# Feed-forward down product as a seven-product 2x2 block multiplication (Winograd's form of Strassen) in two passes

## The chip, the cores and the metric

The kernel runs on one core of a Trainium2 chip. The metric is the device time of one execution in microseconds (us). A core has a matrix engine (TensorE, PE), a vector engine (VectorE, DVE), a scalar engine (ScalarE, ACT), GpSimd (POOL) and SyncE (SP, which issues loads here); sixteen DMA engines move data between HBM and the core's SBUF, and matmuls write to eight PSUM banks. Each engine runs its own list of instructions in the order in which the compiler wrote them; semaphores tie the lists together.

## What is computed

A two-layer decoder trunk over 512 tokens of width 1024 in float32. Each layer has a token mixer (latent attention in layer 0, a gated linear recurrence in layer 1), and then

```python
x = layer_norm(ALPHA * x + mixer(x))
h = x @ w_in                                # 1024 -> 2 * 2816
x = layer_norm(ALPHA * x + (silu(g) * u) @ w_down)   # g, u: halves of h; 2816 -> 1024
x = x + sigmoid(x @ w_gate) * (p @ w_proj)
```

The change concerns the product with `w_down`: 512 tokens x 2816 features times 2816 x 1024, once in each layer.

## The kernel before

**Float32 by three products.** Every operand of a matmul is split into a rounded high part and a low part: `split` (line 178) has ACT copy the value into a float32r tile (`hi`, line 179) and DVE subtract it from the source (`lo`, line 180). `mm3` (line 197) then issues hi·hi, hi·lo and lo·hi (lines 200 to 202). `split_dma` (line 182) makes the low part without DVE: ACT writes the high part (line 184) and its negative (line 185), and a DMA that POOL issues adds the source from HBM to it (line 186), an accumulating DMA.

**Storage.** SBUF tiles come from pools with fixed numbers of buffers: `big`, 14 slots of 8 KB per partition (`slot`, line 167); `ma` and `mb`, five buffers each of 4 KB (`mid`, line 171; `MID_BUFS`, line 49); weights in `raw` (three buffers), `whi` and `wlo` (five each), used by `unit` (line 188). A new tile waits until the buffer that it takes over has had its last reader. PSUM has eight banks: `ps` 3, `sc` 2, `tp` 2, `wg` 1 (line 51). A planner at compile time sets each engine's order: among ready instructions the one that stands first in the program, as far as the buffers allow.

**Gate and up product, `gate_up` (line 380).** This stage stands ahead of the change and already is a Winograd product. Blocks j = 2 to 21 each prepare weights in `prep` (line 389: two loads, two accumulating DMAs, sums on DVE) and run seven products of 12 matmuls of 256 columns in `block` (line 435). It leaves h = silu(g)·u, transposed (features on the partitions), in `hT`: five `big` slots and one `mb` tile for the last two of the 22 feature groups. Beside it the class `Winograd` (line 100) holds the stage's input in eight `big` slots, and x takes two.

**Down product, `ffn` (line 478).** All eight PSUM banks hold the output: four token tiles of 128 (t) by two column halves of 512 (n). For each of the 22 feature groups k a weight tile of 128 x 1024 is loaded and split (`unit`), the 512 tokens of that group are split into an `ma` tile (`hsplit`, line 485), and `part` (line 490) adds 4 x 2 x 3 matmuls of 128x512. The last three groups go token tile by token tile, so that the LayerNorm (`ln_half`, `ln_finish`, lines 324 and 330) of one tile runs beside the matmuls of the next. `ln_finish` defers the transposes of its rows; `flush` (line 310) issues them.

**What follows, `ple` (line 511).** It loads and splits p, runs p·w_proj (48 matmuls), then flushes and runs the gate product in token order through `rows` (line 351).

Of the kernel before, what the change touches and what calls it, by code (L numbers as in the profile page):

```python
# [20 lines left out]
F32 = mybir.dt.float32  # L21
F32R = mybir.dt.float32r
# [18 lines left out]
NF = DFF // P  # L41
# [6 lines left out]
T2 = 4  # L48
# [97 lines left out]
class Builder:  # L146
# [24 lines left out]
    def mid(self, shape, dt=F32, tag="ma"):  # L171
        return self.t4.tile(shape, dt, tag=tag, bufs=MID_BUFS[tag], name=self.nm(tag))
# [175 lines left out]
        return self.small([P, 4], tag="lnst", bufs=6)  # L348


    def rows(self, lhs, units, consume, cut=()):

        for t in range(NT):
# [122 lines left out]
        return hT  # L476

    def ffn(self, l, x, xT, ln):
        hT = self.gate_up(l, xT)
        gb = self.ln_params(ln, True)  # L480
        yT = Pair(self)
        acc = [(self.bank(f), self.bank(g)) for f, g in (("tp", "tp"), ("sc", "sc"), ("ps", "ps"), ("ps", "wg"))]
        NL = 3

        def hsplit(k):
            h = self.mid([P, 2, S], F32R)
            self.split(h[:, 0], h[:, 1], hT[k // 4][:, k % 4, :])
            return h[:, 0], h[:, 1]

        def part(k, t, h, w):  # L490
            for n in range(2):
                self.mm3(acc[t][n], [z[:, t * P:(t + 1) * P] for z in h],
                         [z[:, n * 512:(n + 1) * 512] for z in w], k == 0, k == NF - 1)

        for k in range(NF - NL):
            w, h = self.unit(self.i["ffn_w_down"][l, k]), hsplit(k)
            for t in range(NT):
                part(k, t, h, w)
        last = [(k, self.unit(self.i["ffn_w_down"][l, k]), hsplit(k)) for k in range(NF - NL, NF)]
        for t in range(NT):  # L500
            for k, w, h in last:
                part(k, t, h, w)
            self.flush()
            st = self.new_stats()
            for n in range(2):
                self.ln_half(x, t, n, acc[t][n], st)
            self.ln_finish(x, t, st, gb, yT.sink)
        return yT


    def ple(self, l, x, xT, last):
        nc = self.nc
        praw = self.mid([P, 2, S])
        nc.sync.dma_start(praw, self.i["p"][l])
        pT = (self.mid([P, 2, S], F32R), self.mid([P, 2, S], F32R))
        self.split(pT[0], pT[1], praw)
        pp = Rows(self)
        yT = None if last else Pair(self)
        for n in range(2):
            w = self.unit(self.i["ple_w_proj"][l, n])  # L520
            for t in range(NT):
                ps = self.bank()
                for k in range(2):
                    self.mm3(ps, [z[:, k, t * P:(t + 1) * P] for z in pT], [z[:, k * 512:(k + 1) * 512] for z in w], k == 0, k == 1)
                nc.scalar.activation(pp(t, slice(n * 512, (n + 1) * 512)), ps, AF.Copy)
        self.flush()
        for n in range(2):
            def fin(t, c, ps):
                sg = self.small([P, 512], tag="t2", bufs=T2)[:, c]
                c = slice(n * 512 + c.start, n * 512 + c.stop)  # L530
                nc.scalar.activation(sg, ps, AF.Sigmoid)
# [7 lines left out]
            self.rows(xT, [self.unit(self.i["ple_w_gate"][l, n, u]) for u in range(4)], fin, (NT - 1,) if last and n else ())  # L539
        return yT  # L540


# [196 lines left out]
    def hgrn(self, xT):  # L739
# [9 lines left out]
        for n in range(2):  # L749
            def fin(t, c, ps):  # L750
                a_.activation(vv(t, slice(n * 512, (n + 1) * 512)), ps, AF.Copy)
            self.rows(xT, [self.unit(i["hgrn_w_v"][n, u]) for u in range(4)], fin)

        on = Rows(self)
        W2 = 4 * P
# [146 lines left out]
def layouts(x, p, positions, mla_w_dqkv, mla_q_norm, mla_kv_norm, mla_w_uq, mla_w_ukv, mla_w_o,  # L902
            hgrn_w_in, hgrn_lb_logits, hgrn_out_norm, hgrn_w_o, ffn_w_in, ffn_w_down,
            ln_mix_g, ln_mix_b, ln_ffn_g, ln_ffn_b, ple_w_proj, ple_w_gate):
    a = np.asarray
    c = np.ascontiguousarray
    order = token_order()
    x, p, positions = a(x)[0][order], a(p)[:, 0][:, order], a(positions)[0][order]
    o = {}
    o["x"] = c(x.reshape(NT, P, D).transpose(1, 0, 2))  # L910
    o["xT"] = c(x.T.reshape(KC, P, S).transpose(1, 0, 2))
    o["p"] = c(p.transpose(0, 2, 1).reshape(DEPTH, 2, P, S).transpose(0, 2, 1, 3))
    o["positions"] = c(positions.reshape(NT, P).T)
# [60 lines left out]
```

## Time and profile before

| | |
|---|---|
| median of 3 runs (lowest to highest) | 1300.67 us (1299.48 to 1301.2) |
| the profiled execution: its time, its span | 1299.13 us, 1297.0 us |
| granted TensorE clock | 0.999 |
| down product, layer 0: first matmul | 413.67 us after the span's start |
| down product, layer 0: window 413.67 to 534.00 us | 120.3 us, PE busy 120.3 us |

Times inside the trace count from the start of the span. "Busy" is the time in which an engine had an instruction running; a matmul's recorded length (0.39 us for 128x512) is longer than the distance from one to the next, since they are pipelined, so costs on PE are taken from distances. A wait's "releaser" is the event that ended it, inferred from semaphores.

### The profile page before, as it was taken

What the parts mean: (1) busy time and instruction counts of PE and PEld (TensorE: products, weight loads), DVE (VectorE), ACT (ScalarE), POOL (GpSimd) and SP (SyncE); (2) the same over time, 40 slices, a digit from 0 to 9 for tenths busy, and PEclk for the clock granted to TensorE, in tenths of its full rate; (3) what the DMA queues carried; (4) which work ended last, traced back from release to release, by engine and by line L of the source; (5) the groups of instructions that cost most, each with busy time, mean ns of one, the idle gap of its engine ahead of it and who ended that gap; (6) DMA issues with size and microseconds to landing.
All of it is one profiled execution on the core that took longest, in us unless ns stands there. A gap on an engine that the chain in (4) does not pass through costs nothing.

```text
span 1297.0 us, 20093 instructions
## 1 busy us (share of the span) xinstructions
PE 1272.0 (98%) x7900; PEld 1134.2 (87%) x7900; DVE 809.7 (62%) x1452; ACT 658.5 (51%) x1140; POOL 154.7 (12%) x167
## 2 busy tenths in 40 slices
PE   8999999999999999999999999999999999999998
PEld 8788889999999888888888887888999999888887
DVE  7998488677675332943377776449777676433463
ACT  6666357767764222533334344327767765422352
POOL 0200041111110000100002220023111111000000
PEclk9999999999999999999999999999999999999999
DMA  7213027877884323232412120323888786323231
GB/s 228 68 63 131 26 89 180 210 181 175 186 187 136 98 98 114 85 109 65 133 62 66 66 78 21 115 80 86 213 205 186 181 186 164 119 97 98 94 98 49
DMA packets 47614, 156.45 MB, mean 121 GB/s; under 512 B 5664, under 2 KB 5920, under 8 KB 47264
## 3 DMA queue, kind: packets, MB, share of 16 engines
q1 hardware_dynamic: 36000, 123.71, 29.7%
q0 software_dynamic: 11520, 31.46, 14.0%
q8 instruction: 62, 1.02, 0.3%
q14 instruction: 32, 0.26, 0.1%
HBM read 153.05 MB, written 2.10 MB: 120 GB/s over the span
## 4 chain that ended last, share of the span: by engine, by line
PE 83%; DVE 7%; DMA 4%; ACT 3%; issue 2%; POOL 1%; SPq 0%; DVEq 0%; ACTq 0%; POOLq 0%
PE ps L200 18%; PE ps L201 18%; PE ps L202 18%; PE sc L200 3%; DMA raw<-ffn_w_in 3%; PE sc L201 3%; PE sc L202 3%; PE wg L201 2%; PE wg L200 2%; PE wg L202 2%; PE tp L304 2%; PE sc L812 2%; PE tp L201 2%; PE tp L202 2%; PE tp L200 2%
## 5 line engine op out<-in xcount | busy, mean ns | idle before, releaser
L180 DVE TENSOR_TENSOR wlo<-raw,whi 128x1024 fp32r<-128x1024 f32 (+1 forms) x123 | 148.4, 1209 | 206.2 <-ACT whi L179 204.5
L179 ACT ACTIVATE whi<-raw 128x1024 fp32r<-128x1024 f32 (+1 forms) x135 | 139.5, 1038 | 230.1 <-PE wg L202 125.7
L200 PE MATMUL ps<-big,whi 128*128 128x256 f32 (+1 forms) x768 | 236.9, 308 | 0.0
L202 PE MATMUL ps<-big,wlo 128*128 128x256 f32 (+1 forms) x768 | 236.7, 308 | 0.0
L201 PE MATMUL ps<-big,whi 128*128 128x256 f32 (+1 forms) x768 | 235.5, 307 | 0.0
L200 PE MATMUL ps<-whi,big 128*128 128x512 f32 (+2 forms) x440 | 170.6, 388 | 1.0 <-ACT big L179 1.0
L202 PE MATMUL ps<-whi,big 128*128 128x512 f32 (+2 forms) x440 | 168.2, 382 | 0.0
L201 PE MATMUL ps<-wlo,big 128*128 128x512 f32 (+2 forms) x440 | 168.0, 382 | 0.0
L201 PEld LDWEIGHTS ps<-big,whi 128*128 128x128 f32 x768 | 146.8, 191 | 5.4
L202 PEld LDWEIGHTS ps<-big,wlo 128*128 128x128 f32 x768 | 146.8, 191 | 5.2
L200 PEld LDWEIGHTS ps<-big,whi 128*128 128x128 f32 x768 | 146.9, 191 | 4.8
L200 PEld LDWEIGHTS ps<-whi,big 128*128 128x128 f32 x440 | 82.9, 188 | 15.4 <-ACT big L179 1.2
L202 PEld LDWEIGHTS ps<-whi,big 128*128 128x128 f32 x440 | 82.7, 188 | 15.6
L201 PEld LDWEIGHTS ps<-wlo,big 128*128 128x128 f32 x440 | 82.9, 188 | 14.4
L210 POOL TENSOR_TENSOR rr<-rv,mhalf 128x1 f32<-128x1 f32 (+2 forms) x28 | 26.6, 951 | 481.3 <-DVE rv L208 481.3
L180 DVE TENSOR_TENSOR wlo<-ma,whi 128x1024 fp32r<-128x1024 f32 x40 | 49.0, 1224 | 34.2 <-ACT whi L179 34.2
L202 PE MATMUL ps<-whi,ma 128*128 128x512 f32 x164 | 64.2, 392 | 0.0
L201 PE MATMUL ps<-wlo,ma 128*128 128x512 f32 x164 | 64.2, 392 | 0.0
L200 PE MATMUL ps<-whi,ma 128*128 128x512 f32 x164 | 64.0, 390 | 0.0
L186 POOL DMA_DIRECT2D ma<-ffn_w_in x40 | 34.8, 870 | 234.4 <-DVE big L460 150.8
L439 ACT ACTIVATE part<-ps 128x256 f32<-128x256 f32 x120 | 44.5, 374 | 25.3 <-PE ps L202 24.8
L180 DVE TENSOR_TENSOR mb<-ma,mb 128x1024 fp32r<-128x1024 f32 x40 | 48.9, 1222 | 6.3 <-ACT mb L179 3.4
(309 smaller groups left out, 3071.8 us busy)
## 6 DMA issues: line engine op xcount, KB each, us to landing
raw<-ffn_w_in SPq DMA_DIRECT2D x88, 512.0 KB, 4.6
raw<-ffn_w_down SPq DMA_DIRECT2D x44, 512.0 KB, 3.5
wlo<-ffn_w_in POOLq DMA_DIRECT2D x40, 512.0 KB, 7.3
ma<-ffn_w_in POOLq DMA_DIRECT2D x40, 256.0 KB, 7.0
raw<-ple_w_gate SPq DMA_DIRECT2D x16, 512.0 KB, 3.5
raw<-hgrn_w_fq SPq DMA_DIRECT2D x16, 512.0 KB, 3.5
raw<-mla_w_o SPq DMA_DIRECT2D x8, 512.0 KB, 3.6
raw<-hgrn_w_v SPq DMA_DIRECT2D x8, 512.0 KB, 4.4
```

Source lines behind the costliest of these rows:

```text
L179: self.nc.scalar.activation(hi, src, AF.Copy)
L180: (eng or self.nc.vector).tensor_tensor(out=lo, in0=src, in1=hi.bitcast(F32), op=ALU.subtract)
L186: self.nc.gpsimd.dma_start(lo, src, accum_op=ALU.add)
L200: mm(ps, a[0], b[0], start=start, stop=False, skip_group_check=more)
L201: mm(ps, a[0], b[1], start=False, stop=False, skip_group_check=more)
L202: mm(ps, a[1], b[0], start=False, stop=stop, skip_group_check=more)
L210: nc.gpsimd.tensor_tensor(out=r, in0=v, in1=self.mhalf[:, :n], op=ALU.pow)
L304: self.nc.tensor.transpose(out=ps[:, c * P:(c + 1) * P], in_=src[:, c * P:(c + 1) * P], identity=self.ident)
L439: copy = lambda dst, src: nc.scalar.activation(dst, src[:, :N], AF.Copy)
L812: nc.tensor.matmul(ps[:, c * P:(c + 1) * P], X[:, c * P:(c + 1) * P], pair_view(cs[0][:, :, 1, :], cs[1][:, :, 0, :]), start=True, stop=True)
```

## The change

The 512 x 2816 by 2816 x 1024 product is cut in 2 x 2 blocks: A by token halves (tiles 0, 1 and 2, 3) and feature halves (groups 0 to 9 and 20; 10 to 19 and 21), B by the same feature halves and by column halves. With

S1 = A21 + A22, S2 = S1 - A11, S3 = A11 - A21, S4 = A12 - S2, T1 = B12 - B11, T2 = B22 - T1, T3 = T2 - B11, T4 = T2 - B21

the seven products are P1 = A11·B11, P2 = A12·B21, P3 = S4·B22, P4 = A22·T4, P5 = S1·T1, P6 = S2·T2, P7 = S3·T3, each 256 x 1408 by 1408 x 512 in two PSUM banks.

Pass 1 runs P5, P1, P6, P7 over the features in six blocks b of two group pairs (the block b = 5 has one), in the order 0, 1, 5, 2, 3, 4; all eight banks are in use. T1 and T2 are made by ACT (a negated copy) and an accumulating DMA from HBM (`minus`), the low part of B11 as well (`given`); T3 on DVE. T2 is kept for pass 2: the first in an `ma` tile, the others two by two in a `big` slot (`room`). Then P5 and P1 are copied out by ACT, and DVE forms q = P6 + P1 and c = P7 + q, in four `ma` tiles. Pass 2 runs P4, P2, P3 in the order 5, 0, 1, 2, 3, 4, with T4 on DVE; behind its second block DVE adds what pass 1 gave into x (`early`, 12 instructions). The last two blocks are closed token tile by token tile, first tiles 2 and 3 (P4), then 0 and 1 (P2 and P3). `ple`'s gate product and the value product of layer 1 take the tiles in the order 2, 3, 0, 1, and the array `w_down` is laid out in column halves.

```diff
     def ffn(self, l, x, xT, ln):
+        nc, v = self.nc, self.nc.vector
         hT = self.gate_up(l, xT)
+        wd = self.i["ffn_w_down"][l]
+        NB = 6
+        size = lambda b: 2 if b < NB - 1 else 1
...
+        def minus(dst, z, add):
+
+            nc.scalar.activation(dst, z, AF.Copy, scale=-1.0)
+            nc.gpsimd.dma_start(dst, add, accum_op=ALU.add)
+
+        def made(z, b):
+            w = wt("whi", b), wt("wlo", b)
+            self.split(*w, z)
+            return w
+
+        def given(r, s, b):
+            w = mid(b, "mb", F32R), mid(b, "mb", F32R)
+            self.split_dma(*w, r, s)
+            return w
+
+        def part(ps, t, s, w, b, first, last):
+            for c in range(size(b)):
+                self.mm3(ps, [z[:, c, t * P:(t + 1) * P] for z in s], [z[:, c * 512:(c + 1) * 512] for z in w],
+                         first and c == 0, last and c == size(b) - 1)
+
+        two = lambda f, g: (self.bank(f), self.bank(g))
+        p1, p5, p6, p7 = two("tp", "tp"), two("sc", "sc"), two("ps", "ps"), two("ps", "wg")
+        T2_, room = {}, None
+        order = (0, 1, 5, 2, 3, 4)
+        for n, b in enumerate(order):
+            m = size(b)
+            first, last = n == 0, n == NB - 1
+            r11 = load(0, 0, b)
+            b11 = given(r11, src(0, 0, b), b)
+            hi, lo = (self.slot([P, 4, 2, 256], F32R)[:, :, :m] for _ in range(2))
+            a11, a21, a22 = act(0, 0, b), act(0, 1, b), act(1, 1, b)
+            self.split(hi[:, 0], lo[:, 0], a11)
+            t1 = mid(b, "ma")
+            minus(t1, r11, src(0, 1, b))
+            w1 = made(t1, b)
+            s1 = self.small([P, 2, 256], tag="t2", bufs=T2)[:, :m]
+            v.tensor_tensor(out=s1, in0=a21, in1=a22, op=ALU.add)
+            self.split(hi[:, 1], lo[:, 1], s1)
+            if n == 0:
+                t2 = mid(b, "ma")
+            else:
+                if n % 2:
+                    room = self.slot([P, 2, 1024])
+                t2 = room[:, (n + 1) % 2, :512 * m]
+            T2_[b] = t2
+            minus(t2, t1, src(1, 1, b))
+            w2 = made(t2, b)
+            v.tensor_tensor(out=a21, in0=a11, in1=a21, op=ALU.subtract)
+            v.tensor_tensor(out=a11, in0=s1, in1=a11, op=ALU.subtract)
+            self.split(hi[:, 2], lo[:, 2], a11)
+            t3 = mid(b, "ma")
+            v.tensor_tensor(out=t3, in0=t2, in1=r11, op=ALU.subtract)
+            w3 = made(t3, b)
+            self.split(hi[:, 3], lo[:, 3], a21)
+            for ps, k, w in ((p5, 1, w1), (p1, 0, b11), (p6, 2, w2), (p7, 3, w3)):
+                for t in range(2):
+                    part(ps[t], t, (hi[:, k], lo[:, k]), w, b, first, last)
+
+        keep = lambda: self.mid([P, 2, 512])
+        u, a, q, c = keep(), keep(), keep(), keep()
+        for z, ps in ((u, p5), (a, p1)):
+            for t in range(2):
+                nc.scalar.activation(z[:, t], ps[t], AF.Copy)
+        for z, y, ps in ((q, a, p6), (c, q, p7)):
+            for t in range(2):
+                v.tensor_tensor(out=z[:, t], in0=ps[t], in1=y[:, t], op=ALU.add)
+        p4, p2, p3 = two("sc", "sc"), two("ps", "ps"), two("ps", "wg")
...
+        def early():
+            for t in range(2):
+                add(2 + t, 0, c[:, t], scale=ALPHA)
+                add(2 + t, 1, c[:, t], scale=ALPHA)
+                add(2 + t, 1, u[:, t], stat=True)
+                add(t, 0, a[:, t], scale=ALPHA)
+                add(t, 1, q[:, t], scale=ALPHA)
+                add(t, 1, u[:, t])
+
+        work = []
+        gb = yT = None
+        for b in range(NB):
...
+            b = (5, 0, 1, 2, 3, 4)[b]
+            m = size(b)
+            r21 = load(1, 0, b)
+            t4 = T2_[b]
+            v.tensor_tensor(out=t4, in0=t4, in1=r21, op=ALU.subtract)
+            w4 = made(t4, b)
+            hi, lo = (self.slot([P, 4, 2, 256], F32R)[:, :, :m] for _ in range(2))
+            a12, a22, s2 = act(1, 0, b), act(1, 1, b), act(0, 0, b)
+            self.split(hi[:, 0], lo[:, 0], a22)
+            b21 = given(r21, src(1, 0, b), b)
+            self.split(hi[:, 1], lo[:, 1], a12)
+            b22 = made(load(1, 1, b), b)
+            v.tensor_tensor(out=s2, in0=a12, in1=s2, op=ALU.subtract)
+            self.split(hi[:, 2], lo[:, 2], s2)
+            prods = ((p4, 0, w4), (p2, 1, b21), (p3, 2, b22))
+            if len(work) < NB - 2:
+                for ps, k, w in prods:
+                    for t in range(2):
+                        part(ps[t], t, (hi[:, k], lo[:, k]), w, b, not work, False)
+            work.append((b, hi, lo, prods))
+            if len(work) == 2:
+                early()
         gb = self.ln_params(ln, True)
         yT = Pair(self)
...
+        for t in range(2):
+            close(t, 0)
+            add(2 + t, 0, p4[t], ALU.subtract, stat=True)
+            self.ln_finish(x, 2 + t, st[2 + t], gb, yT.sink)
+        for t in range(2):
+            close(t, 1, 2)
+            add(t, 0, p2[t], stat=True)
+            add(t, 1, p3[t], stat=True)
+            self.ln_finish(x, t, st[t], gb, yT.sink)
         return yT
...
-    o["ffn_w_down"] = c(a(ffn_w_down).reshape(DEPTH, NF, P, D))
+    o["ffn_w_down"] = c(np.stack([halves(a(ffn_w_down)[l]) for l in range(DEPTH)]))
```

`load` issues a plain load by SP into a `raw` tile; `src(i, j, b)` is block Bij's part in HBM, `act(i, half, b)` the part of `hT` with feature half i and token half `half`, and `close` runs the named products of the last two blocks for one token tile and then `flush`.

More of the change, by code (lines that the diff above doesn't have):

```diff
@@ L348, in new_stats, with rows @@
         return self.small([P, 4], tag="lnst", bufs=6)
-    def rows(self, lhs, units, consume, cut=()):
-        for t in range(NT):
+    def rows(self, lhs, units, consume, cut=(), order=range(NT)):
+        for t in order:
             n = 256 if t in cut else 512
@@ L478, in ffn, with src, act @@
     def ffn(self, l, x, xT, ln):
+        nc, v = self.nc, self.nc.vector
         hT = self.gate_up(l, xT)
+        wd = self.i["ffn_w_down"][l]
+        NB = 6
+        size = lambda b: 2 if b < NB - 1 else 1
+        def src(i, j, b):
+            return wd[j, 5 * i + b] if b < NB - 1 else wd[j, 10][:, i * 512:(i + 1) * 512]
+        def act(i, half, b):
+            k = 10 * i + 2 * b if b < NB - 1 else 20 + i
+            return hT[k // 4][:, k % 4:k % 4 + size(b), half * 256:(half + 1) * 256]
@@ new lines, in ffn, with load @@
+        raw = lambda b: self.wp.tile([P, 1024], F32, tag="raw", bufs=3, name=self.nm("raw"))[:, :512 * size(b)]
+        wt = lambda tag, b: self.wp.tile([P, 1024], F32R, tag=tag, bufs=5, name=self.nm(tag))[:, :512 * size(b)]
+        mid = lambda b, tag, dt=F32: self.mid([P, 1024], dt, tag)[:, :512 * size(b)]
+        def load(i, j, b):
+            r = raw(b)
+            nc.sync.dma_start(r, src(i, j, b))
+            return r
+        def minus(dst, z, add):
+            nc.scalar.activation(dst, z, AF.Copy, scale=-1.0)
+            nc.gpsimd.dma_start(dst, add, accum_op=ALU.add)
@@ new lines, in ffn @@
+        keep = lambda: self.mid([P, 2, 512])
[7 more added lines that the diff above has]
+        p4, p2, p3 = two("sc", "sc"), two("ps", "ps"), two("ps", "wg")
+        st = [self.new_stats() for _ in range(NT)]
@@ new lines, in ffn, with add @@
+        L, R = slice(0, 512), slice(512, 1024)
+        def add(t, n, z, op=ALU.add, scale=1.0, stat=False):
+            xs = x(t, (L, R)[n])
+            kw = {"accum_out": st[t][:, n:n + 1]} if stat else {}
+            v.scalar_tensor_tensor(out=xs, in0=xs, scalar=scale, in1=z, op0=ALU.mult, op1=op, **kw)
+        def early():
[6 more added lines that the diff above has]
+                add(t, 1, u[:, t])
@@ new lines, in ffn @@
+        work = []
[3 more added lines that the diff above has]
+            b = (5, 0, 1, 2, 3, 4)[b]
+            m = size(b)
+            r21 = load(1, 0, b)
[18 more added lines that the diff above has]
+                early()
@@ L480, in ffn @@
         gb = self.ln_params(ln, True)
         yT = Pair(self)
[L482 to L502, printed above, removed]
-            self.flush()
[L504 to L507, printed above, removed]
+        def close(t, *ks):
+            for k in ks:
+                for n in (NB - 2, NB - 1):
+                    b, hi, lo, prods = work[n]
+                    ps, _, w = prods[k]
+                    part(ps[t], t, (hi[:, k], lo[:, k]), w, b, False, n == NB - 1)
+            self.flush()
@@ L538, in fin @@
                     self.defer(xs, yT.sink, t, n)
-            self.rows(xT, [self.unit(self.i["ple_w_gate"][l, n, u]) for u in range(4)], fin, (NT - 1,) if last and n else ())
+            self.rows(xT, [self.unit(self.i["ple_w_gate"][l, n, u]) for u in range(4)], fin, (1,) if last and n else (), (2, 3, 0, 1))
         return yT
@@ L751, in fin @@
                 a_.activation(vv(t, slice(n * 512, (n + 1) * 512)), ps, AF.Copy)
-            self.rows(xT, [self.unit(i["hgrn_w_v"][n, u]) for u in range(4)], fin)
+            self.rows(xT, [self.unit(i["hgrn_w_v"][n, u]) for u in range(4)], fin, (), (2, 3, 0, 1))
         on = Rows(self)
```

## Prediction

> **What bounds the kernel now.** I read the page first: busy times, then the shares of the chain that ended last.
>
> ```profile
> span 1297.0 us, 20093 instructions
> ...
> PE 1272.0 (98%) x7900; PEld 1134.2 (87%) x7900; DVE 809.7 (62%) x1452; ACT 658.5 (51%) x1140; POOL 154.7 (12%) x167
> ...
> PE 83%; DVE 7%; DMA 4%; ACT 3%; issue 2%; POOL 1%; SPq 0%; DVEq 0%; ACTq 0%; POOLq 0%
> ```
>
> PE is busy 98% of the span and carries 83% of the chain. But those are means; the stage decides. The table by windows, cut for layer 0 into gate-up blocks, the two windows ahead of the down product, and the down product in halves:
>
> ```profile
> core 0: us, PE busy (x) PEld busy (x) DVE busy (x) ACT busy (x) POOL busy (x), PEclk, DMA share, GB/s
> 353.20:363.30 10.10, 10.10 (x87) 10.10 (x86) 7.24 (x14) 7.11 (x13) 1.75 (x2) 1.00 0.81 182
> ...
> 383.50:393.60 10.10, 10.10 (x86) 10.10 (x86) 5.01 (x11) 6.38 (x12) 1.74 (x2) 1.00 0.85 182
> 393.60:403.60 10.00, 10.00 (x86) 10.00 (x85) 5.25 (x10) 5.51 (x10) 0.00 (x0) 1.00 0.35 107
> 403.60:413.67 10.07, 10.07 (x86) 10.07 (x85) 6.78 (x12) 5.81 (x11) 0.00 (x0) 1.00 0.57 210
> 413.67:473.60 59.93, 59.93 (x267) 49.62 (x266) 20.80 (x25) 17.18 (x22) 0.00 (x0) 1.00 0.30 96
> 473.60:534.00 60.40, 60.40 (x273) 49.52 (x271) 26.33 (x44) 19.40 (x25) 1.98 (x2) 1.00 0.28 88
> ```
>
> In the down product PE never stops (59.93 of 59.93, 60.40 of 60.40), while DVE is busy 20.80 and 26.33 us, ACT 17.18 and 19.40, the DMA engines 0.30 and 0.28. So a matmul taken out here is worth its whole distance, until one of the other three is full. That distance comes from the timeline of PE: the same place of the loop (first matmul into an `sc` bank), one feature group apart.
>
> ```profile
> 415.06 0.39 PE L200 MATMUL sc<-whi,ma 128*128 128x512 f32 x1
> ...
> 420.50 0.39 PE L200 MATMUL sc<-whi,ma 128*128 128x512 f32 x1
> ```
>
> 24 matmuls in 5.44 us: 0.2267 us each. Waits on this side run the other way, ACT and SP waiting for room:
>
> ```profile
> ACT whi L179 <- PE wg L202: 125.7, 37, 4.2
> ...
> DVE ma L398 <- DMA raw<-ffn_w_in: 15.1, 10, 2.6
> ```
>
> ACT waited for PE to give buffers back (125.7 us). The second row matters below: in gate-up DVE came to a load too early 10 times, by up to 2.6 us.
>
> **The matmuls that go.** Before, 22 groups x 24 = 528 a layer. After, seven products x 11 group pairs x 2 token tiles x 3 = 462, of the same form (128x512 moving). 66 x 0.2267 = 14.96 us a layer, 29.9 us in both. This term is a count times a distance; it can only be given back through stalls.
>
> **What ACT and DVE get.** Prices from their timelines, where instructions stand back to back, so that distances count:
>
> ```profile
> 402.35 0.63 ACT L179 ACTIVATE ma<-big 128x512 fp32r<-128x512 f32 x1 [1.05 <-PE ps L202]
> 402.89 1.04 ACT L179 ACTIVATE mb<-ma 128x1024 fp32r<-128x1024 f32 x1
> 403.83 1.04 ACT L179 ACTIVATE whi<-raw 128x1024 fp32r<-128x1024 f32 x1
> ```
>
> ```profile
> 403.22 0.69 DVE L180 TENSOR_TENSOR ma<-big,ma 128x512 fp32r<-128x512 f32 x1
> 403.82 0.42 DVE L462 TENSOR_TENSOR part<-ps,part 128x256 f32<-128x256 f32 x1
> ...
> 404.49 1.22 DVE L180 TENSOR_TENSOR mb<-ma,mb 128x1024 fp32r<-128x1024 f32 x1
> 405.62 0.42 DVE L465 TENSOR_TENSOR mb<-part,part 128x256 f32<-128x256 f32 x1
> ```
>
> ACT: 0.54 us for 512 columns, 0.94 for 1024. DVE: 0.60 and 1.13. A full block of pass 1 costs ACT seven long instructions (B11 twice, T1 and T2 negated, three high parts) and four short ones: 7 x 0.94 + 4 x 0.54 = 8.7 us. DVE: three low parts and T3, four short low parts, S1 to S3: 4 x 1.13 + 7 x 0.60 = 8.7 us. PE: 48 x 0.2267 = 10.9 us. Both fit, at 80%. A full block of pass 2: ACT 4 x 0.94 + 3 x 0.54 = 5.4, DVE 3 x 1.13 + 4 x 0.60 = 5.8, PE 36 x 0.2267 = 8.2 us. So in steady state they cost nothing, being beside PE; without that cover pass 1 alone would put some 48 us a layer on the path.
>
> **The accumulating DMAs.** Three in a block of pass 1, one in pass 2. Rows from gate-up, which has the same kind (the instructions of line 186; the DMA queues between 353.2 and 393.6 us; the end of the last block's preparation):
>
> ```profile
> L186 POOL DMA_DIRECT2D wlo<-ffn_w_in x40: 857/870/1042, 194.5 to 1086.5; - x40
> ...
> DMA to landing us min/median/max: 5.5/7.2/9.3
> ```
>
> ```profile
> q0 software_dynamic: 1152, 3.15, 44.4%
> q1 hardware_dynamic: 1152, 4.19, 35.9%
> ```
>
> ```profile
> 384.78 1.04 ACT L185 ACTIVATE wlo<-whi 128x1024 fp32r<-128x1024 f32 x1
> ```
>
> ```profile
> 386.23 0.87 POOL L186 DMA_DIRECT2D wlo<-ffn_w_in  x1 [1.47 <-ACT part L439]
> ```
>
> From issue to landing 7.2 us, at most 9.3. On the engines, 0.444 x 40.4 us / 3.15 MB x 0.524 MB = 2.98 us for an accumulate of 512 KB, 0.359 x 40.4 / 4.19 x 0.524 = 1.81 us for a plain load. ACT's negation ended at 385.82, POOL issued at 386.23: a hand-over of 0.4 us. POOL issues 24 a layer x 0.87 = 21 us in a stage where it has nothing else until the LayerNorm rows; SP issues 18 loads instead of 22. Neither is on the path.
>
> The start is covered. The `w_down` loads began 39 us ahead of the stage:
>
> ```profile
> 374.52 24.63 SPq L191 DMA_DIRECT2D raw<-ffn_w_down  x5
> ```
>
> The last gate-up accumulate is issued at 386.23; from 393.6 on the DMA engines are at 0.35 and 0.57, DVE busy 12.0 and ACT 11.3 of 20.1 us (of which four units of the old down product fall away). The first block's chain, load, T1, T2, T3, is about 4 + 2 x (1 + 7.2) + 1.2 + 2.3 = 24 us long and can start at 375: in time for 413.67.
>
> Where it can break is buffers. **Place A**, pass 1: `big` has 14 slots, 2 hold x and 5 hold h, so 7 are free. The first three blocks take 2 each, `room` 1. The fourth block's T2 needs the second `room`; the first block's two slots go to the fourth block's own parts, so `room` waits until PE ends the second block, 2 x 10.9 = 21.8 us into the stage. PE wants that T2 after the half block (5.4) and P5 and P1 of the fourth (5.4), 10.9 us later. The chain is 1.04 negation + 0.4 + 7.2 landing + 1.06 high + 1.22 low = 10.9 us: no slack at the median, 2.1 short at 9.3, 5.1 short with another accumulate (2.98) in front. Bounds 0 and 5.1; I take 2.1, since this stage's DMA load is above the one that gave the median.
>
> The Trainium skill ("DMA: Bandwidth & Descriptors", section "Anatomy of one DMA — SWDGE (gpsimd) path") has a fit of 2.0 us plus bytes over 436 GB/s for a DMA on this path, 3.2 us for 512 KB; by it place A would have 4 us to spare and cost nothing, and the forecast would be 4 us lower. The trace, with 5.5 us as the least, speaks against using it for accumulates.
>
> **Place B**, pass 2. The additions of pass 1's results are on DVE:
>
> ```profile
> L327 DVE SCALAR_TENSOR_TENSOR big<-big,ps x22: 674/688/689, 142.7 to 1236.8; 128x512 f32<-128x512 f32 x22
> ```
>
> From the end of pass 1 DVE has c (2 x 0.60), the second block's slot-bound splits (4 x 0.60), `early` (12 x 0.69 = 8.3) and then the third block's low parts of T4 and A22 (1.7; 2.9 if T4 itself isn't made earlier): 13.6 to 14.8 us. PE comes to the third block after 18 + 36 matmuls, 12.2 us. It stalls 1.4 to 2.6 us; 4.9 if the second block's T4 and its low part (2.3) slip behind as well, 0 if `early` is put later. I take 2.0. Behind `early` in DVE's queue stand the low parts for the remaining blocks; DVE regains 8.2 - 5.8 = 2.4 us a block.
>
> At nothing: copying P5 and P1 out (four ACT copies) and q are covered by P6 and P7 of the last block (5.4 us); c (1.2) by P4 and P2 of the half block (2.7); uncovered they would be 1.2. The last tiles close 2.7, 2.7, 5.4 and 5.4 us apart instead of 4.1, with DVE's part a little smaller (6 additions for 8); the last LayerNorm is hidden as before by the 48 matmuls of `ple` (10.9 us), and the new token order has the early tiles first.
>
> Sum: 29.9 - 2 x (2.1 + 2.0) = 21.7 us off. The profiled execution took 1299.13 us, so 1277.4; it lies 1.5 us under the median of 1300.67, so about 1279 against the median. With both stalls at nothing 1270.8, with both at their upper bounds (10.0 a layer) 1290.8; its own range is 1272 to 1289.
>
> **Rivals.** *All hidden*: the planner fills every gap, 1270.8. For it: PE waited for no accumulate at all before. Against: slack of zero at place A.
>
> *The DMA engines become the bound*: a pass 1 block needs 3 x 2.98 + 1.81 = 10.75 us of them in PE's 10.9 us, a share of 0.99, where the rows show 0.81 and 0.85. If 0.85 is the most, the block takes 12.6 us, at 0.81 13.3. With the first block prepared ahead 4.5 blocks are exposed: 8 to 11 us a layer instead of A, so 1300.67 - 29.9 + 16 to 22 + 4 = 1291 to 1297, priced at 1294, up to 1302 if B adds to it. Against: pass 1's accumulates can run ahead into windows at 0.35 and 0.57, so that some 41 us of DMA work is left for 54 us.
>
> *ACT stands in line behind the accumulates* (slower). In gate-up only PE reads an accumulated tile; now ACT must split T1 and T2 right after landing, twice in every block, and what is behind in its list (negations, B11, the next block) waits too. ACT has 10.9 - 8.7 = 2.2 us of slack in a block and the gain is 14.96 / 5.5 = 2.7 us a block; beyond 4.9 us of waits in a block, 2.45 per accumulate, the change loses. At half of the median landing (3.6 us each) a block takes 8.7 + 7.2 = 15.9 us, 5.0 too long, 27.5 us a layer: 1300.67 - 29.9 + 55 = 1326. For it: the 10 waits of DVE on loads of up to 2.6 us show that the planned order can come to data too early. Against: the accumulate issued at 386.23 was for a block that PE began at 403.6, so preparation ran a block ahead; with weights two blocks deep, T1's landing lies before its split's buffer is free.
> The Trainium skill ("TensorE: Matmul & The Clock Gate", section "Architectural detail: the array is 16× 32×32, not 1× 128×128") says that ACT and DVE take their queues strictly first in, first out, which is the rule that speaks against this change; nothing in the trace contradicts it.
>
> That the change doesn't do what it says I leave at no chance: the matmuls are counted.
>
> **How the numbers follow.** Forecast 0.49; all hidden 0.12; DMA bound 0.17 (0.11 faster, 0.05 no change, 0.01 slower); ACT in line 0.22. About 0.2% (2.6 us) is what a measurement of this kernel can tell from no change. Faster by more: 0.49 + 0.12 + 0.11 = 0.72; within 0.05; slower 0.01 + 0.22 = 0.23. The range from 1270 to 1306 holds all but most of the last case.
>
> **What would show it.** Right: PE's matmul count down by 132; in pass 1 PE with one gap of about 2 us ahead of P6 of the fourth block, released by T2's low part, and one of about 2 us at the third block of pass 2, released by DVE; ACT and DVE busy near 80% in pass 1. All hidden: no gap. DMA bound: share above 0.9 throughout pass 1, landings well over 9 us, gaps of 2 us in every block. ACT in line: idle times of ACT ahead of the splits of T1 and T2 ended by a DMA, over 2.45 us each. I am wrong if PE loses over 10 us a layer, or if a gap shows at the start of the stage.

## The result, and the profile after

The changed kernel takes 1339.32 us (median of 4 runs, 1338.22 to 1340.34) against 1300.3 us for the kernel before on the same chip: a ratio of 1.03, 95% interval 1.0282 to 1.0318. The change costs 39 us where 22 us of gain were forecast. The rival on the slower side, "ACT stands in line behind the accumulates", had been priced at 1326 us.

The profiled execution took 1340.34 us. Its page, from the span, the busy times and the chain that ended last:

```profile
span 1338.5 us, 20202 instructions
...
PE 1267.8 (95%) x7768; PEld 1120.8 (84%) x7768; DVE 912.3 (68%) x1608; ACT 751.9 (56%) x1276; POOL 196.4 (15%) x215
...
PE 66%; DMA 10%; issue 9%; DVE 8%; ACT 5%; POOL 1%; SPq 0%; POOLq 0%; DVEq 0%; ACTq 0%
```

The matmuls fell by 132, as counted. But PE's share of the chain fell from 83% to 66%, DMA's rose from 4% to 10%, and "issue" (time in which an engine waited for nothing that the profile shows) from 2% to 9%: a tenth of the time is now landings that somebody waits for. The window of pass 1 of layer 0 (264 matmuls, into P5, P1, P6 and P7; the columns are those of the table by windows above):

```profile
418.39:502.12 83.73, 69.31 (x266) 52.77 (x265) 50.19 (x74) 48.19 (x69) 13.88 (x16) 0.92 0.63 126
```

264 matmuls at 0.2267 us would be 59.85 us; pass 1 takes 83.73. No engine is full: DVE is busy 50.19 us, ACT 48.19, the DMA engines 0.63. The waits of this window (engine, line, releaser: us in total, times, longest) say what PE is short of:

```profile
DVE ma L558 <- DMA big<-ffn_w_down: 22.7, 5, 7.1
...
ACT whi L179 <- DMA big<-ffn_w_down: 18.1, 5, 6.0
...
ACT whi L179 <- DMA ma<-ffn_w_down: 10.4, 3, 4.3
...
PE sc L200 <- ACT whi L179: 6.6, 3, 4.8
...
PE ps L200 <- ACT whi L179: 3.7, 2, 2.7
...
PE sc L201 <- DVE wlo L180: 2.1, 3, 0.8
ACT whi L179 <- PE wg L202: 2.0, 1, 2.0
PE ps L201 <- DVE wlo L180: 1.9, 3, 0.9
```

Read the first two rows of ACT first: ACT, ahead of the high part of T2 (`big`) and of T1 (`ma`), waited eight times for an accumulate, 28.5 us in all, 3.6 us each. PE waited for those same high parts (`sc` is P5, which takes T1; `ps` is P6, which takes T2). DVE, ahead of T3, waited for T2's landings as well (the row of line 558, 22.7 us). The row of `wg` is the other half of the picture: ACT waited for room only once. Before, waiting for room was its main wait; now it is hardly ever ahead. ACT's waits of this window have no row of line 509 at all: no negation waited for a raw load or for a buffer to put T1 or T2 in.

ACT's timeline shows the order that does it. `raw` to `ma` is T1's negation, `ma` to `big` T2's, and each `whi` is the high part of what has just landed:

```profile
459.28 1.04 ACT L509 ACTIVATE ma<-raw 128x1024 f32<-128x1024 f32 x1
...
466.39 1.06 ACT L179 ACTIVATE whi<-ma 128x1024 fp32r<-128x1024 f32 x1 [2.11 <-DMA ma<-ffn_w_down]
467.36 1.04 ACT L509 ACTIVATE big<-ma 128x1024 f32<-128x1024 f32 x1
...
474.18 1.06 ACT L179 ACTIVATE whi<-big 128x1024 fp32r<-128x1024 f32 x1 [3.74 <-DMA big<-ffn_w_down]
475.14 1.04 ACT L509 ACTIVATE ma<-raw 128x1024 f32<-128x1024 f32 x1
```

T1's negation of the next block stands in ACT's list behind T2's high part of this one, so the next accumulate can't be issued before this one has landed and been split. From negation to negation is 475.14 - 459.28 = 15.86 us, where PE needs 10.9. This chain closes on ACT alone: twice a negation with its hand-over to POOL (1.45 and 1.44 us; POOL issued at 460.73 and 468.80), a landing (5.66 and 5.38) and a high part (0.97 and 0.96). DVE's wait for the same landing of T2 hangs beside it. The landings themselves were better than forecast; for the 24 accumulates of line 510, four of them of half the size:

```profile
DMA to landing us min/median/max: 4.0/5.6/7.2
```

On PE's side, the end of the half block's P7 (`wg`) and P5 of the fourth block (`sc`):

```profile
446.36 0.39 PE L202 MATMUL wg<-whi,big 128*128 128x512 f32 x1
451.59 0.65 PE L200 MATMUL sc<-whi,big 128*128 128x512 f32 x1 [4.84 <-ACT whi L179]
452.85 0.79 PE L201 MATMUL sc<-wlo,big 128*128 128x512 f32 x1 [0.61 <-DVE wlo L180]
453.44 0.63 PE L202 MATMUL sc<-whi,big 128*128 128x512 f32 x1
453.87 0.63 PE L200 MATMUL sc<-whi,big 128*128 128x512 f32 x1
...
459.53 0.39 PE L200 MATMUL tp<-mb,big 128*128 128x512 f32 x1
459.75 0.39 PE L201 MATMUL tp<-mb,big 128*128 128x512 f32 x1
```

PE stood still for 5.23 us and then ran at half speed: 0.43 us from matmul to matmul at 453.44, 0.22 again at 459.53. The granted clock (the column behind POOL's) and the DMA share behind it agree:

```profile
446.60:452.00 5.40, 0.56 (x2) 0.19 (x1) 0.90 (x2) 1.52 (x2) 0.85 (x1) 0.98 0.97 181
452.00:456.00 4.00, 3.38 (x8) 2.48 (x8) 0.80 (x1) 3.97 (x6) 0.87 (x1) 0.50 0.39 58
```

So pass 1's excess of 23.9 us is made of PE's own waits for high and low parts (6.6 + 3.7 + 2.1 + 1.9 = 14.3 us), of 23 matmuls behind two of the gaps that stand 0.43 instead of 0.23 us apart (4.6 us), and of 5.0 us around the waits, where the distance from matmul to matmul is longer than the wait (5.23 us across one of 4.84). Gap and half speed at 446.36 together cost 7.4 us. The Trainium skill ("TensorE: Matmul & The Clock Gate", section "What's actually happening") says that the clock is halved after at least one idle window of about 3.4 us and is whole again after at least about as much sustained work. The trace agrees for the 5.23 us here, and the return took 5.1 us of work without a gap (453.44 to 458.56). The trace also has half speed without a gap of 3.4 us: distances of 3.07 and 1.65 us with one matmul between them (from 489.62 on) were followed by 11 slow matmuls. A single distance of 2.98 us (402.35 to 405.33, below) was followed by none.

Two smaller losses have the same root or lie beside it. At the end of gate-up, ACT takes up T2 of the first block, and behind it in its list stand copies of PSUM that PE needs. ACT's and PE's timelines:

```profile
396.86 1.06 ACT L509 ACTIVATE ma<-ma 128x1024 f32<-128x1024 f32 x1 [4.38 <-DMA ma<-ffn_w_down]
...
403.95 1.06 ACT L179 ACTIVATE whi<-ma 128x1024 fp32r<-128x1024 f32 x1 [2.71 <-DMA ma<-ffn_w_down]
404.92 0.64 ACT L439 ACTIVATE part<-ps 128x256 f32<-128x256 f32 x2
```

```profile
405.33 0.38 PE L200 MATMUL ps<-big,ma 128*128 128x256 f32 x1 [2.71 <-ACT part L439]
```

T2's negation reads T1, so it waited 4.38 us for T1's accumulate. T2's high part then waited 2.71 us for T2's, and PE 2.71 us for the copy right behind that. Pass 1 starts 418.39 us into the span, 4.7 later than before (413.67); 3.5 of them came here, and 1.3 us were there already at the same matmul 247 us into the span, ahead of gate-up, a place that varies from -1.2 to +2.1 us among the profiles of the runs below. And in pass 2, ACT's timeline again:

```profile
540.59 1.06 ACT L179 ACTIVATE whi<-raw 128x1024 fp32r<-128x1024 f32 x1 [5.16 <-DMA raw<-ple_w_proj]
541.56 1.13 ACT L335 ACTIVATE t<-big,lnst 128x1024 bf16<-128x1024 f32 x1
```

Here ACT waited for a load of the next stage's weights, while the square for the LayerNorm, which PE needs soon, stood behind it. The DMA engines were full at that point (e7 below moves the load that shares them):

```profile
530.00:540.00 10.00, 9.15 (x41) 7.27 (x40) 6.80 (x12) 2.45 (x3) 0.65 (x1) 1.00 1.03 331
```

The account of layer 0: 4.7 later at the start, 23.9 in pass 1, 7.8 in pass 2 (54.66 us against 46.9 for its 198 matmuls and the transposes of two token tiles), less 15.0 for the matmuls: 21.4 us; measured at the layer's end, 21.1. Layer 1: 6.7 + 24.1 + 4.9 - 15.0 = 20.7; measured 20.4. Together 41.5, the difference of the two spans (1338.5 - 1297.0).

### The profile page after: what moved, and what is told of

Same layout as the page of the kernel before. It is cut to its first block, busy times and chain, and to the rows that moved or that the text cites. A ratio compares the mean times of both kernels' runs of the same rounds, so it can differ in the third digit from the quotient of the medians.

```text
span 1338.5 us, 20202 instructions
## 1 busy us (share of the span) xinstructions
PE 1267.8 (95%) x7768; PEld 1120.8 (84%) x7768; DVE 912.3 (68%) x1608; ACT 751.9 (56%) x1276; POOL 196.4 (15%) x215
## 4 chain that ended last, share of the span: by engine, by line
PE 66%; DMA 10%; issue 9%; DVE 8%; ACT 5%; POOL 1%; SPq 0%; POOLq 0%; DVEq 0%; ACTq 0%
PE ps L200 16%; PE ps L201 16%; PE ps L202 16%; DMA big<-ffn_w_down 3%; DMA raw<-ffn_w_in 3%; PE sc L200 2%; PE sc L201 2%; PE wg L201 2%; PE sc L202 2%; PE wg L200 2%; PE wg L202 2%; DMA ma<-ffn_w_down 2%; DMA raw<-ple_w_proj 2%; PE tp L304 2%; PE sc L942 2%
## 5 line engine op out<-in xcount | busy, mean ns | idle before, releaser
L200 PE MATMUL ps<-whi,big 128*128 128x512 f32 (+2 forms) x528 | 208.6, 395 | 6.2 <-ACT whi L179 6.2
L201 PE MATMUL ps<-wlo,big 128*128 128x512 f32 (+2 forms) x528 | 205.8, 390 | 4.0 <-DVE wlo L180 3.9
L202 PE MATMUL ps<-whi,big 128*128 128x512 f32 (+2 forms) x528 | 205.1, 388 | 0.0
L179 ACT ACTIVATE whi<-raw 128x1024 fp32r<-128x1024 f32 (+1 forms) x103 | 104.7, 1022 | 102.3 <-PE ps L202 35.7
L180 DVE TENSOR_TENSOR wlo<-raw,whi 128x1024 fp32r<-128x1024 f32 (+1 forms) x91 | 108.3, 1192 | 73.5 <-ACT whi L179 71.9
L180 DVE TENSOR_TENSOR wlo<-ma,whi 128x1024 fp32r<-128x1024 f32 (+1 forms) x68 | 81.1, 1192 | 64.0 <-ACT whi L179 64.0
L200 PEld LDWEIGHTS ps<-whi,big 128*128 128x128 f32 x528 | 101.1, 192 | 26.2 <-ACT whi L179 8.3
L201 PEld LDWEIGHTS ps<-wlo,big 128*128 128x128 f32 x528 | 101.2, 192 | 25.4 <-DVE wlo L180 7.4
L202 PEld LDWEIGHTS ps<-whi,big 128*128 128x128 f32 x528 | 100.8, 191 | 19.1
L179 ACT ACTIVATE whi<-ma 128x1024 fp32r<-128x1024 f32 (+1 forms) x68 | 69.7, 1025 | 39.4 <-DMA ma<-ffn_w_down 28.7
L200 PE MATMUL sc<-whi,big 128*128 128x512 f32 (+1 forms) x104 | 42.1, 408 | 14.6 <-ACT whi L179 14.6
L180 POOL TENSOR_TENSOR wlo<-raw,whi 128x1024 fp32r<-128x1024 f32 x12 | 29.6, 2475 | 152.1 <-ACT whi L179 152.1
```

Source lines behind the costliest of these rows:

```text
L179: self.nc.scalar.activation(hi, src, AF.Copy)
L180: (eng or self.nc.vector).tensor_tensor(out=lo, in0=src, in1=hi.bitcast(F32), op=ALU.subtract)
L200: mm(ps, a[0], b[0], start=start, stop=False, skip_group_check=more)
L201: mm(ps, a[0], b[1], start=False, stop=False, skip_group_check=more)
L202: mm(ps, a[1], b[0], start=False, stop=stop, skip_group_check=more)
```

## The experiments

The theory: ACT's place in line. The landings of T1 and T2 lie in series on ACT, and a block takes ACT's own work plus two waits. The rivals: the DMA engines are full, and the loss would be there whoever waits; or the gaps come from buffers (place A); or ACT and DVE simply have too much work. The table holds all eight runs; "pass 1" is the distance from the first to the 265th matmul in layer 0 and layer 1.

| kernel | median us (runs) | ratio to before, interval | pass 1, us |
|---|---|---|---|
| changed | 1339.32 (4) | 1.03, 1.0282 to 1.0318 | 83.7, 84.0 |
| e1_cut | 1279.12 (2) | 0.9845, 0.9816 to 0.9873 | 59.9, 59.9 |
| e2_dve_sums | 1284.64 (2) | 0.9887, 0.9823 to 0.9952 | 59.9, 59.9 |
| e3_pool_sums | 1306.09 (4) | 1.0052, 1.0032 to 1.0072 | 68.0, 68.6 |
| e4_order | 1296.81 (8) | 0.9979, 0.9968 to 0.9991 | 67.2, 65.2 |
| e5_dve_ln | 1276.0 (4) | 0.9815, 0.9797 to 0.9832 | 59.9, 59.9 |
| e6_dve_ln_pool0 | 1275.91 (4) | 0.9815, 0.98 to 0.9831 | 59.9, 59.9 |
| e7_acc_ln | 1333.18 (2) | 1.0258, 1.0232 to 1.0283 | 83.6, 83.3 |
| e8_t1_dve | 1315.96 (2) | 1.0125, 1.0091 to 1.0159 | 69.3, 69.2 |

The kernel before, timed again beside e1 to e4, took 1299.44 us, beside e5 to e8 1300.04.

**e1_cut**: all instructions and DMAs stay, but nothing in pass 1 reads T1 or T2. (PE still reads B11's low part, which is accumulated too.)

```
-            w1 = made(t1, b)
+            w1 = made(r11, b)
...
-            minus(t2, t1, src(1, 1, b))
-            w2 = made(t2, b)
+            minus(t2, r11, src(1, 1, b))
+            w2 = made(r11, b)
...
-            v.tensor_tensor(out=t3, in0=t2, in1=r11, op=ALU.subtract)
+            v.tensor_tensor(out=t3, in0=r11, in1=r11, op=ALU.subtract)
```

> The same instructions and the same DMAs as the changed kernel, but in pass 1 no engine waits for a sum: the products P5 and P6 take B11's split in place of T1's and T2's, the negation for T2 reads B11 in place of T1, and T3 is B11 - B11 (so P5, P6 and P7 are not the reference's; T2 is still read in pass 2). Theory, ACT stands in line behind the accumulates: the 24 us that pass 1 loses in a layer and most of the 4.7 us ahead of it go, and the half clock behind the long gaps with them: 1339 - 2 x 28 = about 1283 us, pass 1 near its 60 us of matmuls. Rival 1, the DMA engines are full: their work is unchanged at 10.75 us in a block, so pass 1 stays at 75 us or more and the time at 1320 to 1339. Rival 2, buffers (room for T2, weights): they are unchanged too, so 1325 or more.

Measured 1279.12 us. Pass 1 of layer 0:

```profile
414.20:474.10 59.90, 59.90 (x267) 49.62 (x266) 51.31 (x76) 48.21 (x69) 13.91 (x16) 1.00 0.87 183
```

PE has no gap left, with the same work on ACT (48.21 us), DVE (51.31) and POOL, and with the same DMAs in less time: a share of 0.87. The buffers are as many, though T1's is free sooner, having no reader left. That buffers weren't it, ACT's waits above show (no row of line 509). So neither the DMA engines nor the amount of work made the loss; the reading of what was just accumulated did. Pass 1 starts at 414.2 instead of 418.39: the delay at gate-up's end goes with it. This is what the change would have brought if the landings of T1 and T2 had been hidden in pass 1. That it is the prediction's time as well is luck: its 8.3 us over the 1270.8 without stalls lie at neither place that the prediction priced, but late in pass 2 (51.2 and 51.0 us against 46.9), where PE itself waits 2.63 and 2.42 us for an accumulate (`mb`, B21's low part).

**e2_dve_sums**: T1 and T2 by a plain load and a subtraction on DVE.

```
         def minus(dst, z, add):
...
-            nc.scalar.activation(dst, z, AF.Copy, scale=-1.0)
-            nc.gpsimd.dma_start(dst, add, accum_op=ALU.add)
+            nc.sync.dma_start(dst, add)
+            v.tensor_tensor(out=dst, in0=dst, in1=z, op=ALU.subtract)
```

> T1 and T2 from plain loads (SP) and one subtraction on DVE each, in place of ACT's negated copy and the accumulating DMA. ACT loses 1.9 us in a block and waits for no accumulate, DVE gets 2.3 us more, 11.0 us in PE's 10.9; DMA work falls to 8.4 us. Theory (ACT in line): pass 1 near 62 to 66 us with DVE as its bound, 1290 to 1300 us in all. Rival 1 (DMA engines full) also expects a gain, of the share from 0.99 to 0.77: 1290 to 1310. Rival 2 (buffers): no gain, 1330 or more.

Measured 1284.64 us, two runs (1281.14 and 1288.15; the profile is of the second), less than any case expected. Pass 1 of layer 0:

```profile
413.54:473.41 59.87, 59.87 (x267) 49.56 (x265) 59.05 (x84) 40.42 (x60) 6.10 (x7) 1.00 0.64 180
```

DVE's 59.05 us fill the pass, and PE still has no gap: the plain load needs no predecessor, so it is issued as soon as its buffer is free, and the subtraction costs 1.2 us of an engine in place of a landing. What is left is at the ends. ACT's timeline in pass 2, and DVE's at the end of gate-up in layer 1:

```profile
511.79 1.06 ACT L179 ACTIVATE whi<-raw 128x1024 fp32r<-128x1024 f32 x1 [5.14 <-DMA raw<-ple_w_proj]
512.75 1.13 ACT L335 ACTIVATE t<-big,lnst 128x1024 bf16<-128x1024 f32 x1
```

```profile
1090.37 1.23 DVE L510 TENSOR_TENSOR ma<-ma,raw 128x1024 f32<-128x1024 f32 x1 [6.71 <-DMA ma<-ffn_w_down]
```

The first is the wait for `ple_w_proj` again. The second is the theory's own wait on another engine: in layer 1 DVE stood in line for 6.71 us ahead of the first block's T1, and gate-up's end came 1.9 us later by it.

**e3_pool_sums**: the same, with the subtractions on GpSimd.

```
+            nc.sync.dma_start(dst, add)
+            nc.gpsimd.tensor_tensor(out=dst, in0=dst, in1=z, op=ALU.subtract)
```

> As with the sums on DVE, but the two subtractions on GpSimd (2.5 us each by its low parts of 128x1024, 5 us of 10.9 in a block), which has nothing else in pass 1. ACT and DVE wait for GpSimd in place of a DMA: 2.5 us in place of 5.6. Theory: pass 1 near 61 to 64 us, 1282 to 1295 in all, below the version on DVE. Rival 2 (buffers): no gain. If DVE's instructions get longer beside GpSimd, both engines slow down and the time is 1300 or more.

Measured 1306.09 us, 0.5% slower than before. GpSimd's and DVE's timelines in pass 1:

```profile
440.36 5.38 POOL L510 TENSOR_TENSOR big<-big,ma 128x1024 f32<-128x1024 f32 x1
...
446.30 2.95 POOL L510 TENSOR_TENSOR ma<-ma,raw 128x1024 f32<-128x1024 f32 x1
449.33 2.71 POOL L510 TENSOR_TENSOR big<-big,ma 128x1024 f32<-128x1024 f32 x1
```

```profile
446.91 2.89 DVE L180 TENSOR_TENSOR big<-big,big 128x512 fp32r<-128x512 f32 x1
449.73 3.39 DVE L180 TENSOR_TENSOR wlo<-big,whi 128x1024 fp32r<-128x1024 f32 x1
453.04 1.21 DVE L180 TENSOR_TENSOR wlo<-ma,whi 128x1024 fp32r<-128x1024 f32 x1
454.17 0.68 DVE L180 TENSOR_TENSOR big<-t,big 128x512 fp32r<-128x512 f32 x1
```

The low part of 512 columns takes 2.89 us beside GpSimd and 0.68 alone, that of 1024 columns 3.39 and 1.21; GpSimd itself takes between 2.7 and 5.4 us in these rows for one shape. The two slow each other down, and the free engine wasn't free. The Trainium skill ("SBUF — State Buffer", section "SBUF: two separate sides") says that GpSimd and a VectorE instruction with two SBUF inputs take turns at a shared pair of ports, one waiting for the whole of the other's instruction; the rows agree, with 2.2 us of waiting in each.

**e4_order**: accumulates as in the change, but written down in another order: T1 of block n+2 and T2 of block n+1 are begun ahead of the splits of block n. To pay for the tiles kept longer, the half block's hi and lo share a slot.

```
+        one(0)
+        one(1)
+        other(0)
         for n, b in enumerate(order):
+            if n + 2 < NB:
+                one(n + 2)
+            if n + 1 < NB:
+                other(n + 1)
```

Here `one(n)` is the load of A11's block and T1's `minus`, `other(n)` the split of B11 and T2's `minus`.

> The sums stay accumulating DMAs, of the same number and size; only the order in the program changes: T1's negation and DMA stand two blocks ahead of the splits that need it, T2's and B11's one block ahead (the half block's parts share one slot, so that the buffers allow it). Theory (ACT in line): each landing of 5 to 7 us now lies behind a block of 10.9 us, so pass 1 falls to 62 to 68 us and the total to 1285 to 1305. Rival 1 (DMA engines full): the DMA work is the same 10.75 us a block, so pass 1 stays above 70 us and the total above 1320.

Measured 1296.81 us: faster than before by 0.2%, the interval just clear of none. Pass 1 of layer 0, and ACT's waits there:

```profile
413.08:480.29 67.21, 63.55 (x267) 51.40 (x265) 53.11 (x78) 46.69 (x69) 11.70 (x14) 0.95 0.76 160
```

```profile
ACT ma L509 <- DMA raw<-ffn_w_down: 6.6, 2, 4.4
ACT big L509 <- DMA ma<-ffn_w_down: 4.8, 3, 3.0
```

With the same accumulates, the same DMA work and the same operations, the order (with the slot that it needs) takes 42 of the 60 us that lie between the changed kernel and e1_cut. The slot alone wasn't run. The rest lies in both passes, 12.6 us over e1 in pass 1 and 8.5 in pass 2: in pass 1 ACT now stands in line elsewhere, ahead of the negations, for the raw load (6.6 us) and for T1 (4.8), and in pass 2 of layer 0 PE waits 5.3 us for the accumulate of B21's low part.

**e8_t1_dve**: T1 by a plain load and DVE, T2 by the accumulate: one landing a block instead of two.

```
-            minus(t1, r11, src(0, 1, b))
+            nc.sync.dma_start(t1, src(0, 1, b))
+            v.tensor_tensor(out=t1, in0=t1, in1=r11, op=ALU.subtract)
```

> The changed kernel with T1 alone from a plain load and a subtraction on DVE; T2 stays an accumulating DMA. ACT has one wait for an accumulate in a block in place of two in series. Theory (two landings in series on ACT set the 15.9 us of a block): a block takes 8 to 12 us of ACT's chain, pass 1 falls from 84 to 62 to 70 us, and the time to 1288 to 1310. Rival (the wait for T2 alone decides, since T3 on DVE hangs on it as well): pass 1 stays above 75 us, 1320 or more.

Measured 1315.96 us, more than the 1288 to 1310 expected, and pass 1 69.25 us, as expected. ACT's timeline, from high part of T2 to the next full block's, and its waits:

```profile
450.98 1.06 ACT L179 ACTIVATE whi<-big 128x1024 fp32r<-128x1024 f32 x1 [2.13 <-DMA big<-ffn_w_down]
...
464.24 1.06 ACT L179 ACTIVATE whi<-big 128x1024 fp32r<-128x1024 f32 x1 [3.43 <-DMA big<-ffn_w_down]
```

```profile
ACT whi L179 <- DMA big<-ffn_w_down: 18.0, 5, 5.9
```

The block takes 13.26 us with one landing in line, where 8 to 12 were expected, against 15.87 with two between the same instructions (458.31 to 474.18), and with none PE's 10.9 decide. T2's wait is as large as in the changed kernel (18.0 and 18.1 us). T1's landing (10.4 us of waits) is out of the line, but ACT waits 7.2 us for DVE's subtraction instead, which stands in DVE's list behind T3 and so behind T2's landing. The rest of the miss is pass 2, 58.0 and 54.4 us, 6.0 more in both layers than in the changed kernel.

**e7_acc_ln and e5_dve_ln**: the LayerNorm rows are loaded right behind `early()` instead of behind the loop, into `ma` tiles of their own instead of a `big` slot; e7 has this edit alone, e5 has it with e2's.

```
                 early()
+                gb = self.ln_params(ln)
-        gb = self.ln_params(ln, True)
```

> The changed kernel with one edit: the LayerNorm parameters loaded right behind the early additions into ma buffers. Sums stay accumulating DMAs. If the tail's two gaps (3.9 us in layer 0, 1.7 in layer 1, with slow matmuls behind) come from loads that crowd there, 2 to 8 us less than 1339, 1331 to 1337; pass 1 is not touched and stays at 84 us. If DVE's own work is the tail, no change.

> T1 and T2 on DVE from plain loads (which alone gave 1284.6 us), and the LayerNorm parameters loaded right behind the early additions into two ma buffers, in place of a big slot at the end of pass 2. There ACT waited 2.4 and 5.1 us in line for the two loads of ple's weights, in a stretch with a DMA share of 1.03, and behind it stood the LayerNorm's squares, for whose transposes PE waited 3.9 us and then ran 7 matmuls at half rate. Theory (ACT in line, here behind plain loads): with 1 MB out of that stretch the two gaps fall by 2 to 4 us a layer with the slow matmuls behind them, 1274 to 1281 us. Rival (the tail is DVE's own work, which is busy all through pass 2): no change, 1283 to 1286.

e7 takes 1333.18 us, 6.1 less than the changed kernel; e5 takes 1276.0, 8.6 less than e2 (whose two runs lie 7 us apart). ACT's wait for `ple_w_proj` in layer 0's pass 2, in the changed kernel and in e7:

```profile
ACT whi L179 <- DMA raw<-ple_w_proj: 5.4, 2, 5.2
```

```profile
ACT whi L179 <- DMA raw<-ple_w_proj: 0.7, 1, 0.7
```

SP issued the load at about the same moment in both (529.3 and 529.9 us), but it landed after 11.2 us in the changed kernel, while none into `raw` took over 5.3 at that place in e7. So this wait was real, but separate: pass 1 of e7 is 83.6 us, as in the changed kernel. About a sixth of the loss (6.1 of 39 us) lay there, and none of it was in the prediction.

**e6_dve_ln_pool0**: e5, with the two subtractions of a layer's first block on GpSimd, where DVE stood in line in e2.

```
-            minus(t1, r11, src(0, 1, b))
+            minus(t1, r11, src(0, 1, b), nc.gpsimd if n == 0 else v)
...
-            minus(t2, t1, src(1, 1, b))
+            minus(t2, t1, src(1, 1, b), nc.gpsimd if n == 0 else v)
```

> As the version with sums on DVE and early LayerNorm parameters, but the first block's two subtractions, which fall into the end of gate-up, on GpSimd: in layer 1 DVE waited 6.7 us in line for the first T1 load, and gate-up ended 3 us late. Theory (an engine in line behind a DMA stops whatever stands behind it): layer 1's gate-up ends on time, 2 to 3 us less. Rival: GpSimd's long instructions beside DVE's slow both, as where all sums were on GpSimd, so 0 to 4 us more.

Measured 1275.91 us against e5's 1276.0: no difference that these runs can tell, where 2 to 3 us less were expected, though layer 1's pass 1 begins at 1102.94 instead of 1105.81 us in the profiles. Of that difference, 2.6 us are there before the end of gate-up in layer 1, where the edit acts; there the profiles show 0.3 us less, and at the same place of layer 0 1.1 us more. It is, with e5, the fastest version here, 1.85% under the kernel before. Its page, and its two passes in layer 0:

```profile
span 1272.1 us, 20197 instructions
...
PE 1243.1 (98%) x7768; PEld 1109.1 (87%) x7768; DVE 932.0 (73%) x1628; ACT 733.7 (58%) x1252; POOL 184.6 (15%) x195
```

```profile
414.60:474.46 59.86, 59.86 (x266) 49.57 (x265) 59.27 (x85) 40.46 (x60) 6.10 (x7) 1.00 0.66 182
474.46:523.40 48.94, 47.59 (x215) 38.44 (x214) 46.79 (x74) 32.81 (x43) 5.90 (x7) 1.00 0.77 217
```

PE is at 98% of the span again. Pass 2 is 48.94 us, 2.0 above its 46.9; with 1.3 in layer 1 that is 3.3 of the 5 us that separate 1275.9 from the 1270.8 of matmuls alone. The rest wasn't traced.

## Why the prediction was wrong

**The matmuls** were right: 132 fewer, 0.2267 us each. In e1, e2 and e6 pass 1 is 59.9 us for 264 of them.

**ACT's and DVE's work** was right in size: 5.5 blocks at 8.7 us are 48 us of each; measured 48.2 and 50.2. **The step that failed stands behind it**: "So in steady state they cost nothing, being beside PE". It compared sums of busy time with PE's time, as if each engine could take its work in any order. ACT takes it in the order written, two landings of that order lie between one negation and the next, and that makes 15.9 us of a block: pass 1 lost 23.9 and 24.1 us. The rival had just this sum, 8.7 us of work and twice 3.6 of waiting; the measured waits are 28.5 us in 8, 3.6 each. That they agree so well is in part luck: the rival's 3.6 was half of a landing of 7.2 us, while the landings took 5.6 with some 2 us of ACT's other work in each.

**Why the rival got only 0.22.** The argument against it was that the accumulate issued at 386.23 ran a block ahead, and that "T1's landing lies before its split's buffer is free". In gate-up nothing on ACT or DVE reads what was accumulated, so ACT can run ahead until it waits for room. In pass 1 it has to read each landing before it can begin the next, so it hardly gets ahead: one wait for room in the whole pass. The row showed that the DMA could be early there, not that ACT's list here would let it be. The prediction said itself that strict order speaks against this change, but didn't follow ACT's new list instruction by instruction.

**Its price** was 13 us low. Pass 1 itself was a little over-priced (48 us in both layers where the rival had 55): the first three blocks have no gap of a microsecond, and the half speed, 4.6 us in layer 0, was not in the sum. Not in it either were the late start (11.4 us in both, 1.3 of them not the change's) and pass 2 (12.7). 48 + 11.4 + 12.7 - 29.9 = 42.2, against 41.5 between the spans.

**The start** was wrong: "in time for 413.67" was worked out for the chain of the DMAs, which was in time. It left out who stands behind the waits of that chain: the copies of gate-up's last results. **Place A** was wrong as a place: the first gap is ahead of P5 of the fourth block, on T1, and there are gaps in each of the last three blocks; its chain of 10.9 us had one accumulate in it, the real one two. **Place B** didn't show: no gap of over 0.6 us at the third block of pass 2. What pass 2 lost, it lost for the greater part to ACT's wait for a load, with the square of the first closed tile's LayerNorm behind it (pass 2 of layer 0: 54.66 us, in e7 49.19). The prediction had the closing of the tiles at nothing and looked only at the last LayerNorm, "hidden as before".

**The DMA engines as the bound** is refuted by e1_cut: the full DMA work of the pass in PE's 59.9 us, at a share of 0.87.

**The range** went to 1306 and left out the case that came. Its own sum had put that case at 1326, and its only ground against it was a row from a stage with another reader.

## What to carry to other kernels

Where an engine issues work and later reads its result, write its list down in order and add up the waits that lie in series between two like places; busy sums say nothing on that. A sum of two HBM tiles by an accumulating DMA can put a landing between two instructions of the same list, which a plain load, issued ahead, and one subtraction don't: here 83.7 against 59.9 us for the pass, although DVE then had 9 us more work. Before changing the order of a list, look at what will stand behind each new wait: it was PSUM copies in gate-up and the LayerNorm's square in the tail.

## What the runs showed of the hardware

A gap in PE costs more than its length: after the 5.23 us, 12 matmuls stood 0.43 us apart, at a granted clock of 0.50, which cost another 2.4 us. GpSimd beside DVE was no free engine: the same low part on DVE took 0.68 us alone and 2.89 beside it. And the DMA engines went to a share of 0.87 at 183 GB/s through a whole pass without costing PE anything.
